# First output projection: weight sums and splits made ahead during the front and the scans, kept in DRAM, and loaded as pairs

## The chip, the cores and the metric

The kernel runs on one core of one Trainium2 chip. The metric is the device time of one execution in microseconds (us). A core has TensorE (PE in the profile: matmuls; PEld: its weight loads), VectorE (DVE), ScalarE (ACT), GpSimd (POOL) and SyncE (SP), each with a queue of its own that it works off in order, and DMA engines that move data between DRAM and the on-chip memory. A DMA is issued from an engine's queue (here SP's, and GpSimd's for those that add to what lies at the target) and then runs by itself.

## What is computed

One step of a small hybrid model: an SSD (Mamba-2) layer, then a pooling layer, over 1024 prompt tokens and 64 sample tokens (1088 columns), with a model width of 1024 and an inner width of 2048. What matters here is the first layer's branch, and of it the last line:

```python
def ssd_branch(h, conv_prev, ssm_prev, w_in, ..., norm_g, w_out):
    zxbcdt = h @ w_in
    ...
    xbc_act = jax.nn.silu(conv)
    ...
    y, new_ssm = ssd_scan(xs, dt, A, Bm, Cm, ssm_prev)
    y = (y + d_skip[:, None] * xs).reshape(b, L, D_INNER)
    gated = (y * jax.nn.silu(z)).reshape(b, L, N_GROUPS, D_INNER // N_GROUPS)
    gated = gated * lax.rsqrt(jnp.mean(gated * gated, axis=-1, keepdims=True) + EPS)
    gated = gated.reshape(b, L, D_INNER) * norm_g
    return gated @ w_out, new_conv, new_ssm
```

The result is gated and added to x; then comes the pooling layer with its own output projection.

## The kernel before

*Number format.* Every float32 product is made of three: an operand is split into hi and lo, and hi·hi, hi·lo and lo·hi are added up. So each weight that TensorE uses has to be split first: a copy to hi on ScalarE, and raw minus hi on VectorE gives lo.

*The output projections* are made by a Strassen scheme of seven half-size products, in the order of ORDER, (2, 6, 3, 5, 1, 4, 7). Each product needs a weight block that is a quadrant of the weights or a sum or difference of two (WBLOCKS: a sum for 2, 5 and 1, a difference for 6 and 7, a plain quadrant for 3 and 4). Each product has four blocks, d = 0 to 3, so there are 28 blocks n = 4 x (place in ORDER) + d, each 128 partitions x 8 x 128 float32 (512 KB). A block is used by 48 matmuls with 128x128 weights, 272 columns wide: 8 rows of the block, two tiles of columns, three products.

*How a weight block is made.* `ow_fetch` loads the quadrant (SP, L1119) into a raw buffer of tag wr (three of them). `ow_add`, if the block is a sum, adds the second quadrant by a DMA that adds to its target (GpSimd's queue, L1137); if it is a difference, ScalarE first negates the raw block in place (L1135, waiting for the load). `ow_split` makes hi on ScalarE (L1148) and lo on VectorE (L1149) into the buffers wh and wl, two of each. `ow_next(n)`, called as TensorE goes through the blocks, splits one further block, adds and fetches what fits. Products send their results with `contribute` (L1168) to the rows of x. Both output projections use these functions: the first with the weights wout, the second, in the pooling layer, with pout (`self.ol` is 0 and 1).

*The stages.* `front` (0 to about 267 us) makes dt, the gates z, and the convolution inputs in eight pairs (the list FRONT; n counts pairs, and names such as B21, T1 or B22 are steps of a fast matrix product inside a pair). Then come eight scans, g = 0 to 7, of four steps p each (`scan`), from 267 to about 860 us; scan 6 begins at about 700 and scan 7 at about 785. A scan's own matmuls are few: transposes (tr, L101), S, and y; they wait for M (a decay matrix), xd and ea from VectorE and ScalarE, and h, the state. The gaps are filled by `fills`: the input projections for the groups ahead (tiles mm), and from the end of scan 6 on the first output products (tiles op, with operands b built from rows of the gated output that come back from DRAM, gyd). The table PACE says how many units of filler go where. After the scans `ssd_out` does the rest of the products until about 996 us, and then the pooling layer runs to the end, with its own output projection.

*What sets the order.* In the scans TensorE's order is pinned as it is written. The order on VectorE, ScalarE, GpSimd and SP is set by the framework's scheduler before the run; on the chip each engine then takes its list in order. Row buffers are 30 slots handed out first-in first-out: a new tile waits for the user before it.

## Time and profile before

The median of three runs is 1621.42 us (1621.29 to 1623.38). The profiled execution took 1624.89 us, of which the profile's span holds 1622.8.

| | before |
|---|---|
| profiled execution, its own time | 1624.89 us |
| span | 1622.8 us |
| granted TensorE clock, mean | 0.985 |
| PE / DVE / ACT / POOL busy | 1581.0 / 1245.1 / 807.6 / 460.3 us |
| chain of work that ended last, PE | 87% |
| DMA moved, hardware queue / software queue | 244.35 / 25.43 MB |

The span is cut into stages by time: up to 267 us the front, to 862 the scans, to 996 the rest of the first output projection. A view of "windows" gives, for each stretch, the busy time of each engine, the clock that TensorE was granted, and the share of the DMA engines' time; a row in which PE is not fully busy, or its clock is under 1, is a place where time can be won. A view of "waits" gives the idle time of an engine by what ended it, as "engine tile line <- engine tile line: us in total, times, longest".

### The profile page before, as it was taken

Reading aid. Unit: us, or ns where it says so; the run is one execution under the profiler, and the core shown is the slowest. Engines: PE = TensorE matmul, PEld = TensorE weight load, DVE = VectorE, ACT = ScalarE, POOL = GpSimd, SP = SyncE. Lnnn points to the kernel's source line nnn. Section 1 sums busy time; section 2 is a strip of 40 time slices with the busy share of each in tenths; the row PEclk is TensorE's granted clock in tenths of the full one; section 3 lists DMA queues with packets and bytes.
Section 4 is the critical chain, followed back from the end, with each engine's and each line's share of the span. In section 5 each row is a group of like instructions: output and inputs, shape, how many; then the busy total and the mean of one; then the engine's idle time right before and its main releaser. Section 6 shows DMA issues by size and latency. Waiting matters only on the chain.

```text
span 1622.8 us, 31026 instructions
## 1 busy us (share of the span) xinstructions
PE 1581.0 (97%) x12399; PEld 1521.3 (94%) x12399; DVE 1245.1 (77%) x1986; ACT 807.6 (50%) x1427; POOL 460.3 (28%) x500
## 2 busy tenths in 40 slices
PE   8999999999999999999799999999999999999997
PEld 6899999999999999998789989999999999999997
DVE  6875476777777777777889878888889777667876
ACT  6653335566657666666654357532323233233363
POOL 0233351212121121213101121665666630000331
PEclk9999999999999999999899999999999999999999
DMA  9422226435454463658599882132333379566673
GB/s 348 164 97 79 98 82 226 138 125 205 149 182 145 155 213 118 211 146 273 141 344 296 211 195 85 71 122 106 113 113 104 105 250 360 145 173 177 159 163 113
DMA packets 103782, 271.74 MB, mean 167 GB/s; under 512 B 17724, under 2 KB 41688, under 8 KB 103640
## 3 DMA queue, kind: packets, MB, share of 16 engines
q1 hardware_dynamic: 95576, 244.35, 43.4%
q0 software_dynamic: 8064, 25.43, 8.9%
q8 instruction: 97, 1.59, 0.4%
q14 instruction: 45, 0.37, 0.1%
HBM read 208.43 MB, written 56.86 MB: 163 GB/s over the span
## 4 chain that ended last, share of the span: by engine, by line
PE 87%; issue 4%; DVE 4%; ACT 2%; DMA 2%; POOL 1%; SPq 0%; DVEq 0%; POOLq 0%; ACTq 0%
PE st L98 29%; PE mm L98 28%; PE op L98 14%; PE y L98 3%; PE pl L98 3%; PE S L98 2%; PE am L98 2%; PE tr L101 1%; PE tr L98 1%; PE ms L98 1%; DMA x<-xT 1%; PE p L98 1%; DMA wr<-wout 0%; DVE rst L1315 0%; PE Z L98 0%
## 5 line engine op out<-in xcount | busy, mean ns | idle before, releaser
L98 PE MATMUL op<-b,w 128*128 128x272 f32 x2688 | 349.6, 291 | 10.9 <-ACT w L1148 5.3
L98 PEld LDWEIGHTS op<-b,w 128*128 128x128 f32 x2688 | 343.3, 191 | 16.2 <-ACT w L1148 6.0
L98 PE MATMUL st<-hh,w 128*128 128x272 f32 x1408 | 273.8, 289 | 0.0
L98 PE MATMUL mm<-hh,wh 128*128 128x364 f32 x720 | 246.8, 343 | 0.0
L98 PE MATMUL mm<-hl,wh 128*128 128x364 f32 x720 | 236.9, 329 | 0.0
L98 PE MATMUL mm<-hh,wl 128*128 128x364 f32 x720 | 236.7, 329 | 0.0
L98 PEld LDWEIGHTS st<-hh,w 128*128 128x128 f32 x1408 | 224.6, 188 | 0.3 <-issue 0.3
L98 PE MATMUL st<-t,w 128*128 128x272 f32 x1584 | 205.3, 287 | 0.0
L98 PE MATMUL st<-hl,w 128*128 128x272 f32 x704 | 203.4, 289 | 0.0
L98 PEld LDWEIGHTS st<-t,w 128*128 128x128 f32 x1584 | 201.0, 188 | 0.0
L98 PEld LDWEIGHTS mm<-hh,wh 128*128 128x128 f32 x720 | 135.8, 189 | 14.0 <-issue 9.7
L187 ACT ACTIVATE w<-wr 128x512 fp32r<-128x512 f32 x88 | 55.5, 631 | 176.3 <-PE st L98 143.0
L98 PEld LDWEIGHTS mm<-hl,wh 128*128 128x128 f32 x720 | 135.9, 189 | 0.7
L98 PEld LDWEIGHTS mm<-hh,wl 128*128 128x128 f32 x720 | 135.8, 189 | 0.0
L98 PEld LDWEIGHTS st<-hl,w 128*128 128x128 f32 x704 | 132.6, 188 | 0.0
L579 POOL TENSOR_TENSOR hd<-h,cd 128x256 f32<-128x256 f32 x56 | 70.7, 1262 | 116.1 <-ACT cd L560 58.4
L1168 DVE SCALAR_TENSOR_TENSOR x<-op,gat,x 128x272 f32<-128x272 f32 (+1 forms) x160 | 72.7, 478 | 34.5 <-PE op L98 31.4
L358 DVE SCALAR_TENSOR_TENSOR raw<-raw,vec,raw 128x1112 f32<-128x1112 f32 x64 | 90.3, 1411 | 10.0 <-ACT raw L356 9.7
L363 POOL COPY ncv<-raw 128x3 f32<-128x3 f32 x32 | 17.1, 533 | 277.9 <-ACT raw L433 267.0
L1148 ACT ACTIVATE w<-wr 128x1024 fp32r<-128x1024 f32 x56 | 59.0, 1054 | 69.1 <-PE op L98 55.0
L946 DVE TENSOR_TENSOR u<-st,u 128x272 f32<-128x272 f32 (+1 forms) x158 | 61.4, 409 | 40.1 <-PE st L98 38.1
L189 POOL TENSOR_TENSOR w<-wr,w 128x512 fp32r<-128x512 f32 x44 | 79.5, 1806 | 37.9 <-ACT w L187 37.6
(272 smaller groups left out, 3216.9 us busy)
## 6 DMA issues: line engine op xcount, KB each, us to landing
wr<-win SPq DMA_DIRECT2D x48, 512.0 KB, 4.0
acb<-acd SPq DMA_DIRECT2D x32, 512.0 KB, 3.8
wr<-pin SPq DMA_DIRECT2D x32, 512.0 KB, 3.5
wr<-wout SPq DMA_DIRECT2D x28, 512.0 KB, 6.5
wr<-pout SPq DMA_DIRECT2D x28, 512.0 KB, 4.6
row<-gyd SPq DMA_DIRECT2D x22, 544.0 KB, 6.7
wr<-wout POOLq DMA_DIRECT2D x20, 512.0 KB, 8.3
wr<-pout POOLq DMA_DIRECT2D x20, 512.0 KB, 5.9
```

What stands on the lines that cost most here:

```text
L98: return self.pin(self.build.nc.tensor.matmul(*a, **k))
L101: return self.pin(self.build.nc.tensor.transpose(*a, **k))
L187: self.nc.scalar.activation(hi, src, AF.Copy)
L189: eng.tensor_tensor(out=lo, in0=src, in1=hi.bitcast(F32), op=ALU.subtract)
L358: nc.vector.scalar_tensor_tensor(out=acc[:, :n], in0=raw[:, k:k + n], scalar=w[k], in1=acc[:, :n], op0=ALU.mult, op1=ALU.add)
L363: nc.gpsimd.tensor_copy(ncv[:, 0:1, :], raw[:, 1024:1027].unsqueeze(1))
L579: nc.gpsimd.tensor_tensor(out=hd, in0=h, in1=cd[:, :, cc].unsqueeze(2).to_broadcast([P, 4, 64]), op=ALU.mult)
L946: nc.vector.tensor_tensor(out=out, in0=x, in1=y, op=ALU.add)
L1148: self.nc.scalar.activation(hi, r, AF.Copy)
L1168: ins = nc.vector.scalar_tensor_tensor(out=x[e][:, a:a + pn], in0=ps[:, :pn], scalar=g, in1=x[e][:, a:a + pn], op0=ALU.mult, op1=ALU.add)
```

## The change

The 28 blocks of the first output projection are no longer made when they are needed. Each is made in two halves ("pieces" of 128 x 4 x 128, 56 in all) beside earlier work:

- `prep_start(n)` takes a slot for each of n pieces and loads one or two quadrant halves (SP, 256 KB each; 96 loads in all).
- `prep_end()` finishes the pieces that were started before: VectorE adds or subtracts the two halves where the block is a sum or difference (40 of 56), ScalarE copies to hi, VectorE makes lo, SP stores hi and lo together (512 KB) to a DRAM tile wpd, and the slot comes free.
- `front` calls them in pairs 1 to 4, and `scan` twice in each step of scans 0 to 5 (the table PREP gives the counts).
- `ow_load()` loads a block's hi and lo from DRAM, 512 KB each, into the seven buffers that were wr (3), wh (2) and wl (2). In the first projection `ow_next(n)` calls it until blocks up to n + 2 are requested. `ow_fetch`, `ow_add` and `ow_split` are left to the second projection.

Gone from the first projection are so 28 loads of wout on SP, 20 adding DMAs on GpSimd, 8 negations and 28 copies on ScalarE, and 28 subtractions on VectorE; the line numbers behind the functions move by two to 48.

```diff
+PREP = {(g, p): (1, 1 if p < 3 or g == 0 else 0) for g in range(6) for p in range(4)}
+OWTAGS = ("wr", "wr", "wh", "wl", "wr", "wh", "wl")
...
+    def prep_start(self, n):
+
+        for _ in range(min(n, 56 - self.prepn)):
+            i, h = divmod(self.prepn, 2)
+            self.prepn += 1
+            blocks, op = WBLOCKS[ORDER[i // 4]]
+            t = self.slots.get("wp", F32R)
+            v = t[:, :1024].rearrange("p (i k m) -> p i k m", i=2, k=4)
+            for j, b in enumerate(blocks):
+                self.nc.sync.dma_start(v[:, j].bitcast(F32), self.io["wout"][i % 4 + 4 * b[0]][:, 8 * b[1] + 4 * h:8 * b[1] + 4 * h + 4, :])
+            self.preps.append((i, h, op, t, v))
+
+    def prep_end(self):
+
+        nc = self.nc
+        for i, h, op, t, v in self.preps:
+            if op:
+                nc.vector.tensor_tensor(out=v[:, 0].bitcast(F32), in0=v[:, 0].bitcast(F32), in1=v[:, 1].bitcast(F32), op=op)
+            nc.scalar.activation(v[:, 1], v[:, 0].bitcast(F32), AF.Copy)
+            nc.vector.tensor_tensor(out=v[:, 0], in0=v[:, 0].bitcast(F32), in1=v[:, 1].bitcast(F32), op=ALU.subtract)
+            nc.sync.dma_start(self.wpd[i][:, :, 4 * h:4 * h + 4, :], v.bitcast(F32))
+            self.slots.free(t)
+        self.preps = []
+
+    def ow_load(self):
+
+        n = len(self.owsplit)
+        if n >= 28:
+            return
+        w = []
+        for i in range(2):
+            tag = OWTAGS[(2 * n + i) % 7]
+            t = self.wp.tile([P, 8, P], F32R, tag=tag, bufs=3 if tag == "wr" else 2, name=self.name("w"))
+            self.nc.sync.dma_start(t.bitcast(F32), self.wpd[n][:, 1 - i])
+            w.append(t)
+        self.owsplit.append(w)
...
     def ow_next(self, n):
 
-        for _ in range(2 if self.ol and n > 21 else 1):
+        while not self.ol and len(self.owsplit) < min(28, n + 3):
+            self.ow_load()
+        for _ in range(0 if not self.ol else 2 if n > 21 else 1):
             self.ow_split()
...
+                if 0 < n < 5 and x in ("B21", "T1", "B22"):
+                    self.prep_end()
+                    if x != "B22":
+                        self.prep_start(2)
...
             if j == 4:
-                for _ in range(2):
-                    self.ow_fetch()
-                self.ow_add()
+                self.ow_load()
...
-        self.ow_split()
-        self.ow_fetch()
-        self.ow_add()
+        self.ow_load()
...
             a, b, c = PACE[g][p]
+            pa, pb = PREP.get((g, p), (0, 0))
+            self.prep_end()
+            self.prep_start(pa)
             self.units(fill, a)
...
+            self.prep_end()
+            self.prep_start(pb)
             self.units(fill, b)
```

Three places show how the engines' lists change. The first is **VectorE in scan 2** (between 440 and 475 us before the change): cb, M (L561) and ea (L562) feed TensorE's y, xd (L545) its S and y, and xbc L587 takes y up. Before:

```order
L548 TENSOR_TENSOR cb_4975<-tr_4950,kc 128x256
L587 SCALAR_TENSOR_TENSOR xbc_4310<-xbc_4310,vec,y_5032 128x256
L561 TENSOR_TENSOR M_4979<-M_4979,cb_4975 128x1024
L587 SCALAR_TENSOR_TENSOR xbc_4531<-xbc_4531,vec,y_5032 128x256
L562 TENSOR_TENSOR ea_5155<-xbc_4132,ea_5155 128x1024
L732 SCALAR_TENSOR_TENSOR xbc_3523<-xbc_3523,vec,rs_5063 128x1088
L732 SCALAR_TENSOR_TENSOR xbc_3742<-xbc_3742,vec,rs_5063 128x1088
L545 TENSOR_TENSOR xd_5137<-tr_5127,tkx 128x2x256
```

With the change:

```order
L550 TENSOR_TENSOR cb_5221<-tr_5196,kc 128x256
L1145 TENSOR_TENSOR wp_5192<-wp_5192 128x512
L563 TENSOR_TENSOR M_5225<-M_5225,cb_5221 128x1024
L1147 TENSOR_TENSOR wp_5192<-wp_5192 128x512
L589 SCALAR_TENSOR_TENSOR xbc_4514<-xbc_4514,vec,y_5285 128x256
L589 SCALAR_TENSOR_TENSOR xbc_4749<-xbc_4749,vec,y_5285 128x256
L1145 TENSOR_TENSOR wp_5868<-wp_5868 128x512
L564 TENSOR_TENSOR ea_5415<-xbc_4322,ea_5415 128x1024
L1147 TENSOR_TENSOR wp_5868<-wp_5868 128x512
L547 TENSOR_TENSOR xd_5397<-tr_5387,tkx 128x2x256 x2
```

Two pieces have come between (a sum, L1145, and a subtraction, L1147, of each): one around M, one around ea, ahead of the next xd; the two operations with rs (L732) have left this place for a later one in the scan.

The second is **ScalarE ahead of scan 7**, about 769 to 788 us before the change: M (L557) is followed by the silu (L394, with its table load) that makes xbc for the scan, and then by b, the hi copies of the output product's operands (L1088). Before:

```order
L356 ACTIVATE raw_8584<-raw_8347,vec 128x1112
L557 ACTIVATE M_8774<-acb_8344,tka_1657 128x128 x4
L557 ACTIVATE M_8774<-acb_8344,tka_1658 128x128 x4
L1135 ACTIVATE wr_8610<-wr_8610 128x1024
L1148 ACTIVATE w_8679<-wr_8597 128x1024
L394 ACT_TABLE_LOAD
L394 ACTIVATE xbc_8583<-xbc_8583 128x1088
L1088 ACTIVATE b_8639<-raw_8600 128x544
```

With the change:

```order
L358 ACTIVATE raw_8971<-raw_8735,vec 128x1112
L559 ACTIVATE M_9148<-acb_8732,tka_1719 128x128 x4
L559 ACTIVATE M_9148<-acb_8732,tka_1720 128x128 x4
L713 ACTIVATE z_8827<-xbc_7869 128x1088
L396 ACT_TABLE_LOAD
L396 ACTIVATE xbc_8970<-xbc_8970 128x1088
L1090 ACTIVATE b_9018<-raw_8984 128x544
```

The negation and the copy of a weight are gone from ahead of the table load, and one square of the gated output (L711 before, L713 now; it stood some 15 rows later) has come there.

The third is **SP's list in scan 2**, at the same time: acb (L519, broadcast decays for M and ea), win (weights of the input projection), rsd and rs (the gate's scale to DRAM and back) and z. Before:

```order
L519 DMA acb_4993<-acd 128x4x256
L132 DMA wr_5175<-win 128x1024
L704 DMA z_5274<-zsd_133 128x1088
L724 DMA rsd_122<-z_4467 4x272
L727 DMA rs_5063<-rsd_122 128x1088
L519 DMA acb_5171<-acd 128x4x256
```

With the change:

```order
L521 DMA acb_5239<-acd 128x4x256
L1137 DMA wp_5868<-wout 128x512
L1137 DMA wp_5192<-wout 128x512 x2
L134 DMA wr_5442<-win 128x1024
L1148 DMA wpd_169<-wp_5192 256x1x512
L726 DMA rsd_122<-z_4685 4x272
L1148 DMA wpd_172<-wp_5868 256x1x512
L729 DMA rs_5316<-rsd_122 128x1088
L1137 DMA wp_5384<-wout 128x512 x2
L521 DMA acb_5431<-acd 128x4x256
```

Loads and stores of pieces now stand between the same transfers; rs and the next acb come behind two stores that wait for VectorE's subtractions, and z has moved behind them.

More of the change, by code (lines that the diff above doesn't have):

```diff
@@ L1123, in ow_src @@
     def ow_src(self, d, b):
-        return self.io[("wout", "pout")[self.ol]][d + 4 * b[0]][:, 8 * b[1]:8 * b[1] + 8, :]
+        return self.io["pout"][d + 4 * b[0]][:, 8 * b[1]:8 * b[1] + 8, :]
+    def prep_start(self, n):
[29 more added lines that the diff above has]
+        self.owsplit.append(w)
     def ow_add(self):
@@ L1143, in ow_split @@
         r = self.owraw[n]
-        if self.ol and ORDER[n // 4] == 7:
+        if ORDER[n // 4] == 7:
             hi, lo = (self.slots.get("w", F32R)[:, :1024].rearrange("p (k m) -> p k m", k=8) for _ in range(2))
@@ L1276, in run @@
             self.b12d = [dr.tile([P, HALF], F32, tag=f"b12d{i}", name=f"b12d{i}") for i in range(8)]
+            self.wpd = [dr.tile([P, 2, 8, P], F32, tag=f"wpd{i}", name=f"wpd{i}") for i in range(28)]
+            self.preps, self.prepn = [], 0
             self.x1d = [dr.tile([P, TOK], F32, tag=f"x1d{i}", name=f"x1d{i}") for i in range(8)]
```

## The prediction

> **What bounds the kernel now.** I read four views in this order: the windows of 100 us, TensorE's own waits, the 10-us windows around each wait, and the timelines of the engines there. The columns of a windows row are stretch, its length, busy time of PE, PEld, DVE, ACT and POOL (with counts), TensorE's granted clock, DMA share and GB/s.
>
> ```profile
> 300.00:400.00 100.00, 99.92 (x844) 92.79 (x843) 77.25 (x108) 64.04 (x131) 23.25 (x37) 1.00 0.48 155
> ...
> 600.00:700.00 100.00, 100.00 (x858) 93.00 (x857) 78.10 (x111) 61.40 (x119) 20.75 (x38) 1.00 0.51 172
> 700.00:800.00 100.00, 88.52 (x673) 82.19 (x672) 76.76 (x116) 66.30 (x126) 20.76 (x30) 0.90 0.69 207
> 800.00:900.00 100.00, 94.28 (x808) 87.95 (x807) 89.21 (x167) 48.28 (x90) 12.89 (x16) 0.97 0.89 286
> 900.00:1000.00 100.00, 94.23 (x729) 92.87 (x728) 83.54 (x160) 55.47 (x85) 18.76 (x36) 0.98 0.69 178
> ```
>
> TensorE is the bound, and it cannot be relieved of work here: the change leaves its matmuls alone. What can be won is idle time and half-clock time. Scans 0 to 5 (about 267 to 700 us) have neither. From 700 to 1000, where the last two scans and the first output projection run, TensorE is idle for 300 - 277.04 = 22.96 us. Its waits there:
>
> ```profile
> PE tr L101 <- DVE xd L545: 5.4, 1, 5.4
> PE op L98 <- DVE w L1149: 3.8, 3, 2.7
> PE S L98 <- DVE xbc L587: 3.6, 1, 3.6
> PE tr L98 <- DVE xd L545: 3.2, 1, 3.2
> PE op L98 <- ACT w L1148: 3.0, 2, 1.9
> PE tr L101 <- ACT xbc L394: 2.9, 1, 2.9
> PE op L98 <- ACT b L1088: 0.9, 1, 0.9
> ```
>
> These seven rows add to 22.8 us: it is the whole idle time. Only 3.8 + 3.0 = 6.8 us of it name the weight split that the change removes. Whether the rest hangs on it too must be read place by place:
>
> ```profile
> 750.00:760.00 10.00, 6.85 (x69) 5.25 (x69) 9.49 (x15) 5.12 (x10) 3.36 (x2) 0.72 1.01 377
> 760.00:770.00 10.00, 10.00 (x84) 9.61 (x85) 8.99 (x15) 9.97 (x18) 3.83 (x5) 0.94 0.69 244
> ...
> 780.00:790.00 10.00, 5.21 (x34) 4.67 (x32) 5.13 (x9) 8.51 (x10) 0.88 (x1) 0.76 0.50 120
> 790.00:800.00 10.00, 6.47 (x30) 5.89 (x31) 9.76 (x18) 6.44 (x10) 1.48 (x2) 0.56 0.63 161
> ...
> 810.00:820.00 10.00, 7.63 (x76) 6.75 (x74) 9.05 (x16) 7.43 (x15) 2.22 (x3) 0.96 0.88 260
> 820.00:830.00 10.00, 8.79 (x56) 7.75 (x58) 9.87 (x20) 5.78 (x13) 1.72 (x3) 0.70 1.04 377
> ...
> 910.00:920.00 10.00, 10.00 (x82) 10.00 (x82) 9.35 (x19) 3.10 (x5) 0.18 (x1) 1.00 0.67 197
> ...
> 980.00:990.00 10.00, 7.26 (x58) 7.04 (x58) 9.52 (x22) 7.10 (x14) 0.45 (x2) 1.00 0.25 81
> 990.00:1000.00 10.00, 10.00 (x69) 10.00 (x69) 9.51 (x20) 6.45 (x12) 1.28 (x5) 0.83 0.54 181
> ```
>
> The clock column falls in or behind a gap. A clock c means half speed for (1 - c)/0.5 of a row; work done at half speed loses half of its time, so a row loses at most (1 - c) x 10 us, and less by half of what it was idle anyway. That is 1.8 to 3.4 us at 750 to 770, 2.6 to 6.8 at 780 to 800, 1.6 to 3.4 at 810 to 830 and up to 1.7 at 990.
>
> The largest place is 780 to 800 (8.3 us idle: the 5.4 and the 2.9). The timelines show its cause (start, length, engine, line, operation, in brackets the idle time before and what ended it); the last row, from the chain, is the transfer:
>
> ```profile
> 770.66 2.45 ACT L557 ACTIVATE M<-acb,tka 128x128 f32<-128x128 f32 x8
> 781.43 1.06 ACT L1135 ACTIVATE wr<-wr 128x1024 f32<-128x1024 f32 x1 [8.32 <-DMA wr<-wout]
> 782.40 1.04 ACT L1148 ACTIVATE w<-wr 128x1024 fp32r<-128x1024 f32 x1
> 784.75 1.11 ACT L394 ACTIVATE xbc<-xbc 128x1088 f32<-128x1088 f32 x1
> 777.26 0.28 DVE L361 SCALAR_TENSOR_TENSOR xbc<-raw,vec,raw 128x64 f32<-128x64 f32 x1
> 783.47 1.23 DVE L1149 TENSOR_TENSOR w<-wr,w 128x1024 fp32r<-128x1024 f32 x1 [4.42 <-ACT w L1148]
> 785.91 1.33 PE L101 MATMUL tr<-kc,xbc 128*128 128x128 f32 x5 [2.89 <-ACT xbc L394]
> 773.31 8.04 DMA wr<-wout
> ```
>
> ScalarE runs in order. The negation of a weight (L1135) stands ahead of the silu for scan 7 (L394), and waits 8.32 us for a weight load that SP issued only at 773.31. The xbc that the silu makes is what the transposes (L101) need, and TensorE goes idle for it at 785.91 - 2.89 = 783.0. VectorE, too, stands still for 4.42 us at a split, with the operations ahead of xd (L545) queued behind it. So these 8.3 us hang on the weights although no weight is named.
>
> **The change part by part.** Removed between 740 and 990:
>
> ```profile
> L1148 ACT ACTIVATE w<-wr x56: 1039/1060/1068, 743.5 to 1585.9; 128x1024 fp32r<-128x1024 f32 x56
> L1149 DVE TENSOR_TENSOR w<-wr,w x56: 1211/1217/1353, 763.4 to 1587.9; 128x1024 fp32r<-128x1024 f32 x56
> 815.36 1.22 DVE L1149 TENSOR_TENSOR w<-wr,w 128x1024 fp32r<-128x1024 f32 x1
> L1135 ACT ACTIVATE wr<-wr x16: 1039/1058/1062, 781.4 to 1576.5; 128x1024 f32<-128x1024 f32 x16
> wr<-wout SPq DMA_DIRECT2D x28, 512.0 KB, 6.5
> wr<-wout POOLq DMA_DIRECT2D x20, 512.0 KB, 8.3
> ```
>
> Half of the splits belong to this projection: 28 x 1.217 = 34 us of VectorE; on ScalarE 28 x 1.060 + 8 x 1.058 = 38 us; and 20 accumulating transfers. What it is worth, place by place:
> - *780 to 800.* With no L1135 or L1148 ahead, the silu waits for its own input. VectorE made that at 777.5 (L361), so the silu moves from 784.75 to about 779 at the latest, with the table load ahead of it, though one square of the gate (L711) now stands ahead too. TensorE went idle at 783, so the transposes should not wait. 8.3 us and a clock loss near 4 us are at stake. VectorE's xd still stands behind a dozen small operations of the output product, so I take **9 us** of the 12.
> - *810 to 830.* TensorE waited 3.6 us for L587, which stood behind the split at 815.36 on a VectorE busy for 9 in 10. That split goes, and one at 802; nothing comes. At stake 3.6 and about 2.5 of clock; half: **3 us**.
> - *The named waits*, in the dense stretch from 860 on: 6.8 us and up to 1.7 of clock at 990. What is late next is the ready load: two of 512 KB for each block of 48 matmuls (about 6.2 us of TensorE), issued up to two blocks ahead, about 12 us, against 6.5 us from issue to landing in the row above. I take **6 us**.
> - *747 to 770.* This wait (3.2) follows the longest wait of VectorE for the gate's scale, rs, on its way back from DRAM (the L732 row below: 5.9 us); its place in VectorE's order stays. **0**.
>
> Together 18 us of the 22.96 idle and 8 to 15 of clock.
>
> Added ahead, in front pairs 1 to 4 and scans 0 to 5: 56 pieces of 128x512. The same shapes stand in the trace:
>
> ```profile
> L187 ACT ACTIVATE w<-sw x66: 615/631/635, 98.1 to 1328.6; 128x512 fp32r<-128x512 f32 x66
> L189 DVE TENSOR_TENSOR w<-sw,w x66: 674/693/1785, 99.0 to 1329.3; 128x512 fp32r<-128x512 f32 x66
> DVE xbc L732 <- DMA rs<-rsd: 18.9, 6, 5.9
> ACT ea L552 <- DMA acb<-acd: 13.1, 9, 3.2
> L579 POOL TENSOR_TENSOR hd<-h,cd x56: 607/1553/1685, 285.0 to 838.1; 128x256 f32<-128x256 f32 x56
> ```
>
> VectorE: 40 sums and 56 subtractions x 0.693 = 66.5 us. ScalarE: 56 x 0.631 = 35 us. A scan of 71 us takes about 7 pieces: 7 x (40/56 + 1) x 0.693 = 8.3 us on VectorE, from 77% to 89%, and 4.4 us on ScalarE, from 64% to 70%. So VectorE does 66.5 - 34 = 32 us more in all, in a stage where TensorE has not waited once. At 910 to 920 VectorE is busy for 9.35 of 10 and TensorE for all 10, at 760 to 770 for 8.99 and TensorE again all 10; at 810 to 820 it is 9.05 and TensorE loses 2.4. So 89% may cost nothing or a wait. Lower bound 0; upper bound one wait like the 3.6 with its 2.5 of clock in each of six scans, 36 us. VectorE's idle time in a scan (22.5% of 71 us, 16 us) is twice what comes, so I take the near end, **2 us** in all.
>
> SP's queue gets 96 loads of 256 KB and 56 stores of 512 KB, about 6.8 MB in a scan, 96 GB/s on top of 155 to 172. A store waits for VectorE's subtraction, and behind it stand acb, rs, z and h0 loads of the scan. If one is late by the 3.2 us that ScalarE has already waited for acb, TensorE's lead has covered it so far. From nothing to 3.2 us in each of six scans, 19 us; near the lower end, **0.5 us**.
>
> The Trainium skill ("SBUF — State Buffer", section on the two separate sides) speaks against the change: a VectorE operation with two SBUF inputs and a GpSimd one that reads SBUF exclude each other for a whole instruction. The L189 row agrees in its longest (1785 ns against 693). By that rule, as an estimate, 96 operations that meet GpSimd in a fifth of cases for half of L579's 1.55 us add 15 us of VectorE time; the rows by themselves, at the median, add none. Spread over the stage it is 2 to 3 us a scan, and still below VectorE's idle time.
>
> The profiled execution took 1624.89 us (span 1622.8 and 2.1 around it): 1624.9 - 18 + 2.5 = 1609.4. It lay 3.5 us above the median of 1621.42; from the median the forecast is **1606 us**.
>
> **The rivals.**
> 1. *Swallowed.* Other work takes over in the same places: xd behind the product's own VectorE work at 780 to 800, L587 at 810, and the ready loads (twice the requests on SP, in order with rows and x1d stores) in place of the split. For it: DMA share 1.04 at 820 to 830. Against it: the accumulating transfers, 8.3 us each, go. It leaves only about 5 us: **1616 us**.
> 2. *Slower.* VectorE falls behind in scans 0 to 5. The pieces stand between cb and M and ahead of ea, which feed the y matmuls; TensorE's order is fixed, so one late y stops everything. At the upper bound above, 36 us against 18: **1639 us**. It decides from 18/6 = 3 us a scan on. Against it: no wait of TensorE at all in 300 to 700.
> 3. *The loads are not ready*, so that the change does not do what it says: the pairs come from DRAM later than the split would have been done. If each of 28 blocks waited 1 us, 28 us against 18: about 1631 us. Against it: 12 us ahead for 6.5 us.
>
> **How the numbers follow.** The forecast's own case, 8 to 27 us gained, gets 0.70; the first rival 0.16, the second 0.10, the third 0.04. Below 26 us of gain (all idle time but the 3.2, and 6 of clock; 1595 us) lies perhaps 0.05; above 1626 most of the last two rivals. So the range is 1595 to 1626. A difference under 0.2% (3.2 us) is about what a measurement of this kernel cannot tell from none. Faster: 0.70 and 0.09 of the first rival, 0.79; within 0.2%: 0.07 of it and 0.02 of the others, 0.09; slower 0.12.
>
> **What would show it.** Right: the 100-us rows from 300 to 700 keep TensorE at 99.9 or more with VectorE at 87 to 90; ScalarE shows no wait near 780; TensorE is idle under 10 us in 700 to 1000, and the clock at 780 to 800 is near 1; the wait near 750 stays. The software queue falls by 20 x 0.524 = 10.5 MB and the hardware queue grows by 25.2 + 29.4 + 29.4 - 14.7 = 69 MB. Wrong: TensorE waits for M, ea, xd or h before 700 with a clock below 1 there (second rival), or for a load of ready weights after 770 (third), or L545 and L587 still stop it at 780 to 830 (first).

## The result, and the profile after

The changed kernel takes 1647.07 us (median of 4 runs, 1646.3 to 1652.09) against 1621.36 us before: ratio 1.0162, 95% interval 1.0141 to 1.0184. It is 25.7 us slower, where the prediction had 15 us faster and a range of 1595 to 1626. The profiled execution took 1647.45 us, its span 1645.5, so 22.7 us more than the span before.

The page of the change, engine line and DMA queues:

```profile
PE 1585.4 (96%) x12399; PEld 1524.2 (93%) x12399; DVE 1275.6 (78%) x2054; ACT 800.3 (49%) x1447; POOL 439.7 (27%) x480
...
q1 hardware_dynamic: 128664, 313.57, 55.9%
q0 software_dynamic: 5184, 14.94, 5.2%
```

The work is what was worked out: the queues moved by +69.2 and -10.5 MB, VectorE does 30 us more, GpSimd 21 less. Only the waits are elsewhere. To see where, both programs are cut at the same events. The first state copy of a scan (VectorE, h<-S) is one; here scans 0, 6 and 7, first before, then with the change:

```profile
284.54 0.41 DVE L576 COPY h<-S 128x256 f32<-128x256 f32 x1
...
711.10 0.42 DVE L576 COPY h<-S 128x256 f32<-128x256 f32 x1
...
798.41 0.42 DVE L576 COPY h<-S 128x256 f32<-128x256 f32 x1
```

```profile
301.55 0.41 DVE L578 COPY h<-S 128x256 f32<-128x256 f32 x1
...
742.40 0.42 DVE L578 COPY h<-S 128x256 f32<-128x256 f32 x1
...
818.01 0.42 DVE L578 COPY h<-S 128x256 f32<-128x256 f32 x1
```

Scan 0 begins 17.0 us late; by scan 6 the delay is 31.3; scan 6 gives back 11.7. In the table each column is a stage between such events, in us longer (+) or shorter (-) than before: the front, scans 0 to 6, scan 7 with the dense rest of the output projection (to the first matmul of pl, the pooling layer), the pl matmuls, and all that follows. The rows below the first are the experiments. All are single profiled executions, within 6.5 us of the medians. The one of the kernel before lay 3.5 us above its median, so the table shows losses too small, and gains too large, by about as much. The two runs of the kernel before with negations moved agree with it to 1 us in the front and 0.3 us in scans 0 to 5; so most of the 3.5 us should lie in scan 6 or behind it.

| run | front | 0 | 1 | 2 | 3 | 4 | 5 | 6 | 7+out | pl | rest | span |
|---|---|---|---|---|---|---|---|---|---|---|---|---|
| before (us) | 284.5 | 69.2 | 72.2 | 70.9 | 70.9 | 71.1 | 72.2 | 87.3 | 197.7 | 49.0 | 577.7 | 1622.8 |
| the change | +17.0 | -0.4 | +4.7 | +6.7 | +2.2 | +1.1 | 0.0 | -11.7 | -1.9 | +4.9 | +0.1 | +22.7 |
| pieces in scans only | -0.5 | +0.4 | +10.1 | +4.4 | +0.6 | +0.8 | +0.4 | -11.8 | -2.0 | +4.9 | +0.7 | +8.1 |
| pieces in front only | +16.2 | -0.4 | 0.0 | 0.0 | 0.0 | -0.3 | +0.2 | -11.2 | 0.0 | +3.4 | -0.5 | +7.4 |
| no loads | +4.5 | -2.3 | +3.9 | 0.0 | +1.8 | +1.7 | -0.1 | -11.4 | +0.7 | +3.4 | +1.4 | +3.5 |
| transfers only | +4.4 | +0.2 | +17.9 | +6.3 | +2.7 | -0.2 | -0.1 | -11.4 | +1.3 | +3.4 | -0.5 | +24.1 |
| 56 pieces in scans 0 to 6 | +0.1 | +0.3 | +11.7 | +0.6 | +4.2 | +2.1 | +5.6 | +1.6 | -2.1 | +3.4 | -0.2 | +27.5 |
| the same, finished later | -0.1 | 0.0 | +3.6 | +7.4 | +1.4 | +1.9 | +3.9 | -11.6 | -2.1 | +4.9 | +2.3 | +11.6 |
| copies, not paced | +59.3 | +4.1 | +16.5 | 0.0 | 0.0 | -0.3 | 0.0 | -11.5 | 0.0 | +4.8 | +1.4 | +74.3 |
| copies, paced, scans | +0.9 | +3.5 | +1.1 | +0.9 | 0.0 | -0.3 | +5.5 | -11.9 | -2.4 | +4.9 | +1.0 | +3.2 |
| operations only, scans | +0.3 | +2.3 | +2.4 | 0.0 | +0.8 | +0.7 | +0.6 | -11.8 | -1.8 | +4.9 | +2.2 | +0.6 |
| scans, half the ready loads | +0.2 | +0.3 | +10.3 | +5.5 | 0.0 | +0.5 | +1.0 | -11.0 | -8.4 | +2.5 | +3.0 | +3.8 |
| scans, stores on GpSimd | +1.4 | +2.2 | +6.0 | +14.4 | +5.9 | +3.1 | -1.1 | -10.7 | -1.6 | +4.9 | +0.4 | +24.8 |
| scans, all on GpSimd | +14.1 | +0.2 | +19.2 | +10.9 | +18.0 | +9.3 | -1.4 | -11.5 | -0.7 | +3.4 | +1.4 | +63.0 |
| before, negations on GpSimd | -0.7 | -0.3 | 0.0 | 0.0 | 0.0 | -0.3 | 0.0 | -5.9 | +3.0 | -0.1 | +5.1 | +0.8 |
| the same, first projection | -1.0 | +0.1 | 0.0 | 0.0 | 0.0 | -0.3 | 0.0 | -6.5 | +2.4 | -0.1 | +1.8 | -3.6 |
| 8 blocks, scans 4 and 5 | -0.4 | -0.3 | 0.0 | 0.0 | +0.2 | +0.7 | +4.4 | -13.6 | -7.3 | +3.4 | 0.0 | -12.9 |
| 8 blocks, scans 2 to 5 | +1.6 | -0.3 | 0.0 | 0.0 | +1.0 | +0.8 | -0.9 | -11.6 | -5.4 | +5.7 | +1.6 | -7.5 |

**The front.** Windows of 100 us (columns as in the prediction), first two of the kernel before, then those of the change:

```profile
100.00:200.00 100.00, 100.00 (x800) 99.07 (x799) 55.33 (x108) 35.90 (x64) 41.91 (x32) 1.00 0.28 98
200.00:300.00 100.00, 100.00 (x770) 98.73 (x769) 66.62 (x104) 48.60 (x87) 30.58 (x35) 1.00 0.44 148
```

```profile
100.00:200.00 100.00, 90.21 (x692) 88.21 (x692) 64.35 (x117) 37.65 (x69) 34.53 (x25) 0.95 0.66 213
200.00:300.00 100.00, 97.85 (x750) 96.87 (x749) 69.21 (x113) 45.26 (x77) 35.75 (x41) 1.00 0.51 173
300.00:400.00 100.00, 100.00 (x819) 93.34 (x818) 83.60 (x123) 68.60 (x145) 23.45 (x33) 1.00 0.74 249
400.00:500.00 100.00, 94.22 (x773) 87.17 (x772) 82.68 (x119) 63.59 (x127) 20.46 (x33) 0.96 0.78 255
...
600.00:700.00 100.00, 97.65 (x788) 89.81 (x778) 83.40 (x118) 65.09 (x139) 21.25 (x33) 0.98 0.70 228
```

VectorE of the change is busy for 64% from 100 to 200, and TensorE is idle for 9.8 us there all the same, where before it was full. The waits of VectorE from 100 to 290 us, those of SP, and a piece of the timeline say why:

```profile
DVE wp L1145 <- DMA wp<-wout: 27.0, 7, 5.5
```

```profile
SPq L1148 <- DVE wp L1147: 29.7, 8, 7.5
```

```profile
154.04 0.78 DVE L948 TENSOR_TENSOR z<-st,u 128x272 f32<-128x272 f32 x2
157.98 0.69 DVE L1145 TENSOR_TENSOR wp<-wp 128x512 f32<-128x512 f32 x1 [3.16 <-DMA wp<-wout]
...
163.97 0.70 PE L100 MATMUL tr<-kc,dt 128*64 128x128 f32 x4 [6.77 <-DVE tka L508]
```

VectorE is not full: it stands still, in order, at a sum whose load has not landed. The small operations that TensorE needs (z, tka) stand behind it. And SP stands still, in order, at a store whose subtraction VectorE has not reached, with the next loads behind it. So a load, the sum that needs it and the store behind the sum wait for each other in turn.

**The scans.** From 290 to 700 us, where TensorE did not wait before, its waits in the change, ScalarE's wait for loads of pieces, and SP's waits:

```profile
PE am L100 <- ACT mp L268: 5.8, 2, 4.0
PE tr L100 <- DVE xd L547: 2.4, 1, 2.4
```

```profile
ACT wp L1146 <- DMA wp<-wout: 20.1, 7, 6.1
```

```profile
SPq L1148 <- DVE wp L1147: 73.0, 23, 8.4
...
SPq L1137 <- DMA wpd<-wp: 38.3, 11, 6.2
...
SPq L615 <- DMA wpd<-wp: 14.6, 7, 4.8
...
SPq L706 <- DMA wpd<-wp: 11.2, 5, 2.5
```

A piece of the chain (start, length, what):

```profile
456.35 5.34 DMA wpd<-wp
...
468.74 4.64 DMA wp<-wout
...
473.50 0.70 DVE wp L1145
...
479.08 0.54 SPq L1148
...
483.39 7.45 DMA wp<-wout
...
490.94 0.18 ACT wp L1146
...
496.73 0.28 ACT mp L268
...
497.06 1.03 PE am L100 x4
```

SP stands 73.0 us at stores of pieces (L1148) that VectorE has not finished. A load of a piece (L1137) waits on SP until the last store out of its slot has landed; so do loads of h0 (L615) and z (L706) that got such a slot. The end of this chain is ScalarE at a piece whose load landed at 490.84, with mp (adaLN) behind it, and TensorE waits 4 us for mp. Transfers of pieces are 17 of the 41 us of this chain by the rows shown (5.34 + 4.64 + 7.45).

**The gain.** TensorE's only long wait in scan 6 of the change, then the windows there:

```profile
PE tr L103 <- DVE xd L547: 3.5, 1, 3.5
```

```profile
802.00:812.00 10.00, 8.80 (x72) 8.61 (x70) 10.00 (x20) 8.52 (x12) 0.00 (x0) 1.00 0.72 231
812.00:822.00 10.00, 7.66 (x79) 6.63 (x79) 9.49 (x19) 3.53 (x9) 1.77 (x1) 1.00 0.49 175
```

Of 8.3 us idle and about 4 of clock, 3.5 idle are left and the clock stays at 1.

**The dense rest.** No weight split is waited for any more, and nothing is gained. TensorE's waits from 818 to 1014 us of the change, the windows at them, and the transfer behind the second:

```profile
PE op L100 <- ACT b L1090: 5.8, 2, 5.0
PE S L100 <- DVE h L698: 4.3, 1, 4.3
```

```profile
840.00:850.00 10.00, 8.06 (x62) 7.59 (x64) 8.70 (x14) 4.96 (x13) 1.24 (x2) 0.67 1.00 369
...
960.00:970.00 10.00, 6.13 (x26) 5.59 (x27) 5.47 (x11) 5.33 (x10) 2.58 (x3) 0.66 0.95 219
```

```profile
946.02 7.41 DMA row<-row
```

The waits for splits went (ready weights are waited for 0.6 us); an operand b whose adding DMA (row<-row, 7.4 us) comes late took their place, with the clock at 0.66 behind it, and in scan 7 the state h took the place of L587. In the pl stage, 4.9 us longer, TensorE waits 1.9 us for ss (L1283) and 1.0 us for wl (L155), for which it did not wait before; every run built on the change is 2.5 to 5.7 us longer there, also those that load half the ready weights or those of 8 blocks only. What makes these late is open.

### The profile page after: what moved, and what is told of

Same layout as the page of the kernel before. It is cut to its first block, busy times and chain, and to the rows that moved or that the text cites. A ratio compares the mean times of both kernels' runs of the same rounds, so it can differ in the third digit from the quotient of the medians.

```text
span 1645.5 us, 31414 instructions
## 1 busy us (share of the span) xinstructions
PE 1585.4 (96%) x12399; PEld 1524.2 (93%) x12399; DVE 1275.6 (78%) x2054; ACT 800.3 (49%) x1447; POOL 439.7 (27%) x480
## 4 chain that ended last, share of the span: by engine, by line
PE 59%; DVE 12%; DMA 11%; issue 10%; ACT 5%; POOL 2%; SPq 1%; DVEq 0%; ACTq 0%; POOLq 0%
PE st L100 22%; PE mm L100 19%; PE op L100 9%; DMA wp<-wout 4%; DMA wpd<-wp 2%; PE y L100 2%; PE am L100 1%; PE S L100 1%; PE pl L100 1%; PE tr L100 1%; PE tr L103 1%; DVE x L1209 1%; PE ms L100 1%; DMA wr<-win 1%; DMA wr<-pout 1%
## 5 line engine op out<-in xcount | busy, mean ns | idle before, releaser
L100 PE MATMUL op<-b,w 128*128 128x272 f32 x2688 | 349.3, 291 | 10.5 <-ACT b L1090 5.8
L100 PEld LDWEIGHTS mm<-hh,wh 128*128 128x128 f32 x720 | 136.6, 190 | 13.8 <-issue 11.2
L581 POOL TENSOR_TENSOR hd<-h,cd 128x256 f32<-128x256 f32 x56 | 77.1, 1376 | 138.1 <-DVE h L582 57.9
L360 DVE SCALAR_TENSOR_TENSOR raw<-raw,vec,raw 128x1112 f32<-128x1112 f32 x64 | 89.6, 1400 | 10.1 <-ACT raw L358 9.9
L559 ACT ACTIVATE M<-acb,tka 128x128 f32<-128x128 f32 x256 | 80.5, 389 | 17.5 <-PE y L100 15.2
L1146 ACT ACTIVATE wp<-wp 128x512 fp32r<-128x512 f32 x56 | 35.0, 629 | 107.6 <-DVE wp L1145 68.4
```

What stands on the lines that cost most here:

```text
L100: return self.pin(self.build.nc.tensor.matmul(*a, **k))
L360: nc.vector.scalar_tensor_tensor(out=acc[:, :n], in0=raw[:, k:k + n], scalar=w[k], in1=acc[:, :n], op0=ALU.mult, op1=ALU.add)
L559: nc.scalar.activation(M[:, r, t], acb[:, r, t], AF.Relu, bias=self.tka[cc][:, col + r:col + r + 1], scale=-1.0)
L581: nc.gpsimd.tensor_tensor(out=hd, in0=h, in1=cd[:, :, cc].unsqueeze(2).to_broadcast([P, 4, 64]), op=ALU.mult)
L1146: nc.scalar.activation(v[:, 1], v[:, 0].bitcast(F32), AF.Copy)
```

## The experiments

Each run is timed against the kernel before on the same chip. Where a run leaves out or changes a part of the computation, its expectation says so.

### Which stage, and which part of a piece

**Pieces in scans only, pieces in the front only.**

```diff
-        for _ in range(min(n, 56 - self.prepn)):
+        for _ in range(min(n, 40 - self.prepn)):
...
-            self.nc.sync.dma_start(t.bitcast(F32), self.wpd[n][:, 1 - i])
+            self.nc.sync.dma_start(t.bitcast(F32), self.wpd[n if n < 20 else n - 8][:, 1 - i])
...
-                if 0 < n < 5 and x in ("B21", "T1", "B22"):
-                    self.prep_end()
-                    if x != "B22":
-                        self.prep_start(2)
```

> The change without its pieces in the front: the scans make 40 pieces (20 blocks), blocks 20 to 27 load the pairs of blocks 12 to 19 once more (same traffic, other numbers). From the traces, scan 0 began 17 us later than before and scans 1 to 4 took 14 us longer, while scan 6 and the dense stretch gave back about 13. If the loss of the front belongs to the pieces there: 1647 - 17 = 1630 us, with TensorE's waits of 120 to 250 us gone. Rival (the loss is a matter of DMA traffic or queues at large and moves elsewhere when the pieces move): over 1640.

```diff
-PREP = {(g, p): (1, 1 if p < 3 or g == 0 else 0) for g in range(6) for p in range(4)}
+PREP = {}
...
+            self.nc.sync.dma_start(t.bitcast(F32), self.wpd[n % 8][:, 1 - i])
```

> The change with its 16 pieces in the front alone, none in the scans; every block from 8 on loads the pair n modulo 8 (same loads in the dense stage, other numbers). If front and scans lose apart from each other: 1647 - 14 = 1633 us, with scans 1 to 4 at their 71 us again and the front still 17 us late. If the scans were slowed only as an after-effect of the front: about 1647 still, or scans still at 73 to 77 us.

Measured: 1633.53 us, ratio 1.0082 (1.0062 to 1.0101), and 1635.27 us, 1.0087 (1.0072 to 1.0102). The front's 17 and the scans' 14 to 17 are separate losses; each stays whole when the other is gone.

**No loads, and transfers only.** The expectations from here on go by letters. W: engines that work in order stand still for loads of pieces. V: the added operations cost their own time on VectorE. S: SP's queue and the slots are what is short. D: the traffic or SP's queue is the loss; later it is split into T, the traffic itself makes other transfers late, and Q, SP is held at the head of its queue by a piece that cannot start.

```diff
-            for j, b in enumerate(blocks):
-                self.nc.sync.dma_start(v[:, j].bitcast(F32), ...)
...
+            c = self.kc[:, :512].rearrange("p (k m) -> p k m", k=4)
             if op:
-                nc.vector.tensor_tensor(out=v[:, 0].bitcast(F32), in0=v[:, 0].bitcast(F32), in1=v[:, 1].bitcast(F32), op=op)
+                nc.vector.tensor_tensor(out=v[:, 0].bitcast(F32), in0=c, in1=c, op=op)
...
```

> The change without the 96 loads of wout: the pieces are made of constants that lie on the chip, with the same VectorE and ScalarE operations and the same stores (other numbers). Theory W: no wait for loads is left, and the 31 us come back, 1612 to 1620 us. Theory V: the operations are all there, 1640 or more. Theory S: part of the loss stays with the stores, which still hold SP until VectorE is done, 1625 to 1640.

```diff
-            for j, b in enumerate(blocks):
+            for j, b in enumerate((blocks * 2)[:2]):
...
-            if op:
-                nc.vector.tensor_tensor(out=v[:, 0].bitcast(F32), ...)
-            nc.scalar.activation(v[:, 1], v[:, 0].bitcast(F32), AF.Copy)
-            nc.vector.tensor_tensor(out=v[:, 0], ...)
```

> The change with the transfers of its pieces alone: loads (two halves for every piece, 112 in place of 96) and stores, no VectorE or ScalarE operation on them (raw halves are stored, other numbers). Theory W (the loss is engines standing still in order for piece loads): no engine waits for a piece now, so nearly all of the 31 us come back, 1612 to 1620 us. Theory D (the traffic of 54 MB or SP's queue is the loss): it stays, 1635 or more. Half of each would be 1622 to 1635; the run without loads left 10 us of loss in front and scans, which this run then gives to the operations or to the stores' wait for VectorE.

Measured: 1628.72 us, 1.0051 (1.0036 to 1.0066), and 1652.66 us, 1.0198 (1.0180 to 1.0216). In the **front** theory W holds: the loss falls from 17 to 4.5 us when there is nothing to wait for, and to 4.4 when nobody waits; what these last 4.5 us are is open. In the **scans** W alone does not explain the loss: with no operation on the pieces (and 112 loads in place of 96) they lose 26.8 us, more than the change's 14.3. Without loads they lose 5.0. The waits of ScalarE, VectorE and SP from 350 to 470 us of the run with transfers only:

```profile
ACT ea L554 <- DMA acb<-acd: 22.9, 4, 8.7
```

```profile
DVE xbc L734 <- DMA rs<-rsd: 9.6, 1, 9.6
```

```profile
SPq L1137 <- DMA wpd<-wp: 28.8, 7, 7.2
SPq L1144 <- DMA wp<-wout: 24.5, 11, 5.9
```

SP stands at pieces for 53 of 120 us, and the scan's own transfers come late behind them: ScalarE waits 22.9 us for acb, VectorE 9.6 for rs.

### Lead, traffic, operations, queue

**A longer lead**, as a pair: all pieces in scans 0 to 6, then the same with every piece finished one call later.

```diff
+PREP = {(g, p): (1, 1) for g in range(7) for p in range(4)}
...
+        held = self.preps[len(self.preps) - self.started:]
+        for i, h, op, t, v in self.preps[:len(self.preps) - self.started]:
...
+        self.preps, self.started = held, 0
```

> All 56 pieces in scans 0 to 6, two in each step, none in the front; numbers as the reference's. It is the partner of the next run. From the run with scans only (1633.5 us, 16 us lost in scans 1 to 4): 1632 to 1640 us, if the price belongs to pieces in scans.

> The same 56 pieces in the same steps of scans 0 to 6, each finished one call (about half a step, 9 us) later, so that its load has longer to land; same operations, same transfers. Theory W: the waits for piece loads go and with them most of the scans' loss, 1615 to 1623 us. Theory V (the operations' own time on VectorE): as its partner, within 3 us. Theory S (slots are short): as its partner or slower, since a piece holds its slot longer.

Measured: 1658.5 us, 1.0227 (1.0206 to 1.0248), far over the 1632 to 1640 expected, and 1640.04 us, 1.0120 (1.0101 to 1.0138). The lead is worth 18 us, 13 of it in scan 6, where pieces stood beside the start of the output product; scans 1 to 5 still lose 18. Waiting for a load is a part, not the whole. In the front a longer lead has no result: with pieces that hold their slots a call longer there, the list of free slots runs empty.

**Traffic that waits for nothing**: copies from DRAM to DRAM in place of the pieces, first as the scheduler puts them, then queued on SP behind the scan's latest acb.

```diff
...
+            for j, b in enumerate((blocks * 2)[:2]):
+                for w in (self.wpd, self.wpe):
+                    self.nc.sync.dma_start(w[i][:, j, 4 * h:4 * h + 4, :], self.io["wout"]...)
```

> The traffic of the pieces without anything to wait for: each piece is four copies of 256 KB from DRAM to DRAM, issued by SP at the places of the loads, with no slot, no engine operation and no wait on another piece (224 copies, 59 MB in and out of the DMA engines; other numbers). The run with transfers alone lost 31 us in front and scans. Theory T (traffic as such: other transfers land later because of it): most of that loss stays, 1640 us or more. Theory Q (SP's queue in order: a piece's load at its head waits for a slot whose last store has not landed, and acb, rs and weights behind it come late): nothing of the pieces waits now, so the loss goes, 1612 to 1622 us.

```diff
...
+            with self.tc.issue_after(self.lastsp):
+                b = blocks[0]
+                for w in (self.wpd, self.wpe):
+                    self.nc.sync.dma_start(w[i][:, h], self.io["wout"][i % 4 + 4 * b[0]][:, 8 * b[1]:8 * b[1] + 8, :])
```

> Scans only, 40 pieces, and of each piece only traffic that waits for nothing: two copies of 512 KB from DRAM to DRAM, queued on SP behind the scan's latest acb load, so that they are spread over scans 0 to 5 as the pieces were (the earlier run without this order issued its copies early and crowded front and scan 0); other numbers. The run with all of the 40 pieces in scans lost 16 us in scans 1 to 5, the one with transfers alone 27. Theory T (traffic as such, acb landing in 5.6 us in place of 3.8): 12 to 27 us lost in the scans, 1628 us or more. Theory Q (SP held at the head of its queue by a piece that waits for its slot, its load or VectorE): under 5 us lost in the scans, 1610 to 1618 us.

**Operations without transfers.**

```diff
-                self.nc.sync.dma_start(v[:, j].bitcast(F32), ...)
...
-            nc.sync.dma_start(self.wpd[i][:, :, 4 * h:4 * h + 4, :], v.bitcast(F32))
+            if i < 2:
+                nc.sync.dma_start(self.wpd[i][:, :, 4 * h:4 * h + 4, :], v.bitcast(F32))
...
```

> Scans only, 40 pieces, and of each piece only its VectorE and ScalarE operations, on constants (stores of the first two blocks alone, no loads of wout; the output product loads those two blocks over and over; other numbers). Theory V (VectorE's added 0.7-us operations are late for TensorE): the 16 us of the scans stay in good part, 1622 us or more. If the operations are hidden, as the prediction had it (2 us): 1609 to 1615 us.

Measured: 1697.85 us, 1.0466 (1.0442 to 1.0490): the copies, with nothing to hold them back, crowded into the front, so that this run tells only that crowded traffic is dear. Paced: 1628.31 us, 1.0060 (1.0039 to 1.0081). Operations only: 1625.21 us, 1.0035 (1.0021 to 1.0049). A window in scan 1 and the landing of acb and win from 290 to 700 us of the paced copies, then the same window with the operations only:

```profile
350.00:420.00 70.00, 69.54 (x586) 64.06 (x585) 52.52 (x73) 42.36 (x90) 17.20 (x25) 1.00 0.85 272
```

```profile
acb<-acd SPq DMA_DIRECT2D x23, 512.0 KB, 4.6
wr<-win SPq DMA_DIRECT2D x23, 512.0 KB, 9.1
```

```profile
350.00:420.00 70.00, 68.42 (x577) 63.12 (x576) 61.79 (x91) 46.62 (x93) 17.93 (x25) 1.00 0.53 176
```

With the DMA engines at 0.85 TensorE keeps 69.5 of 70 us; with VectorE at 88% (61.79 of 70) it keeps 68.4. Over scans 0 to 5 traffic alone loses 10.7 us and operations alone 6.8, together about what the whole pieces lose (16.7); traffic alone so lies between what T and what Q gave. But not at the same place: in scans 1 and 2, where the whole pieces lose 14.5, traffic loses 2.0 and operations 2.4. Some 10 us there come with neither part by itself, while transfers that wait for slots and for each other lose 24.2 in the same two scans. That the waiting makes the difference is argued, not shown: the copies also stood at a better place in SP's queue, behind the scan's acb, and the two were not tried apart.

**Pieces off SP's queue**: stores, then loads too, issued by GpSimd.

```diff
-            nc.sync.dma_start(self.wpd[i][:, :, 4 * h:4 * h + 4, :], v.bitcast(F32))
+            nc.gpsimd.dma_start(self.wpd[i][:, :, 4 * h:4 * h + 4, :], v.bitcast(F32))
```

> As the run with pieces in scans alone (1633.5 us, 16.7 us lost in scans 0 to 5), with the pieces' stores issued by GpSimd and not by SP: same operations, same bytes, but SP is no longer held until VectorE has subtracted. Theory Q: much of the 16.7 comes back, 1620 to 1627 us, unless GpSimd's own work (hd, which the state h needs) is then late behind the stores. Theories T and V: no gain, 1632 or more.

> The same with the pieces' loads on GpSimd's queue too, so that nothing of a piece stands in SP's queue (104 issues of about 0.9 us each on GpSimd, whose idle time in scans 1 to 5 is over 75%). Theory Q: acb, rs and weights are in time, 1616 to 1624 us if hd is not held up; if GpSimd, in order too, is held by pieces as SP was, TensorE waits for h in place of the rest, 1630 or more. Theory T: 1630 or more with no wait for h.

Measured: 1651.12 us, 1.0191 (1.0154 to 1.0228), and 1690.49 us, 1.0429 (1.0410 to 1.0448). Both are worse, against theory Q as I had put it. SP's waits from 290 to 700 us with the stores on GpSimd:

```profile
SPq L1137 <- DMA wpd<-wp: 63.1, 13, 8.2
...
SPq L615 <- DMA wpd<-wp: 36.2, 9, 8.5
...
SPq L706 <- DMA wpd<-wp: 28.2, 5, 9.7
```

SP is no longer held by VectorE, but by slots: the stores leave GpSimd late, so a slot comes back late, and the next loads into it, of pieces, h0 and z, hold SP for 127 us (51 us in the run with pieces in scans only, which has the stores on SP; 64 in the change). TensorE's longest wait in total is for mp (12.7 us); for h, whose hd GpSimd makes, it waits 4.4. So the queue is the place where it shows, and what looks short is the slot, held from the load until the store has landed. This is read from the waits; a run with more slots was not made. With the loads on GpSimd too, TensorE waits for h (24.9 us), whose hd stands behind pieces there.

### The gain

**The negation alone**, in the kernel before: made by GpSimd, in both projections, then in the first alone.

```diff
-            self.nc.scalar.activation(self.owraw[n], self.owraw[n], AF.Copy, scale=-1.0)
+            self.nc.gpsimd.tensor_scalar(out=self.owraw[n], in0=self.owraw[n], scalar1=-1.0, scalar2=None, op0=ALU.mult)
```

> The kernel before, with one edit: the negation of a weight block (L1135) is made by GpSimd, whose adding DMA waits for it anyway, in place of ScalarE. It tests what the prediction said of 780 to 800 us: that the silu of scan 7 stood behind a negation that waited for its load. If so, it gains there by itself what the change gained (scan 6 was 11.7 us shorter in the change's trace): 1607 to 1613 us. If the gain came from the removal of the splits or of the weight's loads: 1617 to 1622.

> The kernel before with the negations of the first output projection alone on GpSimd (the earlier run moved those of the second projection too, and lost 5.1 us at the end there). Its scan 6 was 5.9 us shorter and the dense stretch 3.0 longer: 1620 - 3.6 = 1616 to 1618 us. If the end's loss had another cause: 1623 to 1626 again.

Measured: 1626.04 us, 1.0031 (1.0019 to 1.0044), and 1621.38 us, 0.9990 (0.9975 to 1.0006). Scan 6 gets 5.9 and 6.5 us shorter, half of what the change gains there, but the kernel gains nothing: 8.0 and 4.1 us are lost again from scan 7 on, and the profiled execution of the kernel before lay 3.5 us above its median. Neither run met its expectation. TensorE's longest wait from 690 to 1000 us in the second:

```profile
PE tr L101 <- DVE xd L545: 5.5, 1, 5.5
```

The wait for the silu went, the wait for xd stayed whole. Splits and their transfers still stand on its way, which was not tried apart. So the negation named by the trace was not the only thing in line.

**Half the ready loads** in the dense rest: a block's hi also serves as its lo.

```diff
-        for i in range(2):
+        for i in range(1):
...
-            w.append(t)
+            w += [t, t]
```

> As the run with pieces in scans alone (1633.5 us), but in the first output projection a block's hi is loaded once and used as its lo too: half the ready loads, 14.7 MB less between 750 and 990 (other numbers). In that run, as in the change's own trace, the dense stretch waited 4.5 to 5 us at about 955 for an operand b whose adding DMA row<-row came late, and 4.3 at about 835 for the state h. If the doubled weight loads make row<-row late: the wait at 955 goes, dense stretch 5 to 8 us shorter, 1626 to 1629 us. If not: 1632 to 1635.

Measured: 1628.35 us, 1.0035 (1.0015 to 1.0055). Its waits for b from 800 to 1010 us:

```profile
PE op L100 <- ACT b L1090: 0.9, 2, 0.5
```

The wait of 4.5 us is gone, and the dense rest and pl are 8.8 us shorter than with both loads (-8.4 and +2.5 against -2.0 and +4.9). By the medians it is about 7.5 us (1.0035 against 1.0082). So the loads of the ready pairs are what ate the gain there; whether by their bytes or by their requests in SP's queue was not tried apart.

**A smaller change**: the first 8 blocks (products 2 and 6) ahead, 16 pieces; the rest as before. First with the pieces in scans 4 and 5 (shown), then in scans 2 to 5 at half the rate.

```diff
+PREP = {(g, p): (1, 1) for g in (4, 5) for p in range(4)}
+READY = 8
...
+        if not self.ol and n == 0:
+            self.owraw, self.owtags, self.owadd = [None] * READY, [None] * READY, READY
...
+            if not self.ol and len(self.owsplit) < READY:
+                self.ow_load()
+                if n < READY - 4:
+                    continue
+            else:
+                self.ow_split()
```

> A smaller change: only the first 8 blocks (products 2 and 6) are made ahead, 16 pieces in scans 4 and 5, two in each step, none in the front; blocks 8 to 27 are fetched, added and split as before; numbers as the reference's. In the change's trace scans 4 and 5 lost 1.1 us with 14 pieces and scan 6 gained 11.7, while the dense stretch and the handover to the pooling layer lost 3.0. If gains and losses belong to their places: 1620 - 11.7 + 1 to 3 = 1609 to 1612 us. If pieces anywhere cost 0.3 us each as in scans 1 and 2: 1615 to 1620.

> As the run before, with the 16 pieces spread over scans 2 to 5, one in each step. If the loss comes from pieces close behind each other (a load that waits for the slot of the piece before): less loss than two in a step, 1607 to 1612 us. If scan 2 is dear as such (it lost 6.7 us in the change's trace): 1612 to 1618.

Measured: 1615.67 us, ratio 0.9958 (0.9944 to 0.9972), and 1616.39 us, 0.9966 (0.9954 to 0.9979). Both are faster than the kernel before, by 0.4 and 0.3%, and than the changed one; neither reached the 1612 us or less that they had in their better cases. The profiled execution of the first lay 4.0 us under its median, so its row in the table flatters it. Scan 6 keeps its 11.6 to 13.6 us, the pieces cost 5.1 us in scans 4 and 5, and 0.9 when spread over scans 2 to 5, and the dense rest, with the old way of making weights, is better than with ready pairs. The windows of the first of them from 600 to 800:

```profile
600.00:700.00 100.00, 99.17 (x849) 91.98 (x848) 87.22 (x123) 63.11 (x126) 23.15 (x38) 1.00 0.79 261
700.00:800.00 100.00, 94.31 (x773) 88.06 (x773) 86.11 (x135) 69.14 (x137) 18.37 (x26) 0.98 0.72 246
```

At the same DMA share (0.79) and a fuller VectorE (87%) than in the change's scans, TensorE is idle for 0.8 us in 100. It is not free for that: scan 5 of this run is 4.4 us longer, and from 700 to 710, at its end, TensorE is busy for 8.51 us at a clock of 0.83.

## Why the prediction was wrong, step by step

- *What bounds the kernel, and the idle 22.96 us*: right (the three rows add to 277.03, so 22.97).
- *780 to 800, 9 us*: right. 8.3 idle and 4 of clock, less the 3.5 left, is 8.8. The cause was half named: with the negation alone moved, scan 6 is about 6 us shorter, and the wait for xd stays.
- *747 to 770, 0*: wrong to the good side. The wait of VectorE for rs fell from 5.9 to 3.2 us, and TensorE's 3.2 to 0.3. What made rs earlier was not tried apart.
- *810 to 830 and the named waits, 3 + 6 us*: failed. "What is late next is the ready load" was the wrong answer: loads were in time (0.6 us of waits). Late next was the operand b, and half the ready loads made it early; with pl, whose part is open, the balance is +3.0 in place of -9. The first rival had the result. It named the ready loads, by their requests on SP, but xd and L587 beside them: the wait for xd fell from 5.4 to 3.5 us and that for L587 went.
- *Added ahead, 2 + 0.5 us*: the step that decides, and it is 31. Two things in it failed. First, the working priced the pieces in the **scans** alone; the front got no term and no reason for it. In the windows of before TensorE is full there and VectorE at 55 to 67%, which looks as safe as the scans. It cost 17.0. Second, the working asked whether VectorE has *time* for the pieces ("VectorE's idle time in a scan is twice what comes"), and in the main it has: operations alone cost 6.8 us over six scans, which is over three times the 2 but half of the loss; paced traffic alone cost 10.7. It didn't ask what stands in order *behind* a piece that waits. SP's wait for a store was named in it and put at 0.5 us "near the lower end", because TensorE's lead had covered such waits before; the upper end written there, 19 us, is near the 14.3 of scans 0 to 5, in part by luck: it was six times a late acb, and TensorE's named waits there are for mp, behind ScalarE at a piece whose load is late, and for xd.
- *The second rival* had the sign and the size (36 us), with VectorE too full before M and ea as its mechanism. VectorE is at 83% in place of 89, and the waits of VectorE, ScalarE and SP at pieces are for loads, slots and each other.
- *The port that VectorE and GpSimd share* (the Trainium skill, "SBUF — State Buffer", the two separate sides): the rule's estimate was 15 us of VectorE time. The pieces' sums average 798 ns and the subtractions 732 at medians of 684 and 686, so 40 x 0.114 + 56 x 0.046 = 7 us: it shows, at half the size. All ten of the 96 that took over 0.72 us ran beside an operation of GpSimd, eight of them in the front. It decides little: with the same operations and no loads the front lost 4.5 us.

Still open: how the change's own 14 us in the scans divide among traffic, operations and waits for each other. The parts were measured alone, and they don't fall on the same scans as the whole.

## What to carry to other kernels

Work moved into a stage with idle engines is not priced by its busy time alone but by what stands behind it in order while it waits: for its load, for the slot, for the store before it; look for that on the DMA-issuing queue as well as on the engines. A buffer that holds load, work and store in turn is taken for the sum of all three, and where buffers are shared, every other user of them is late too. When waits in a stage all go away and its length doesn't change, look at what the new traffic makes late; and move only the blocks whose wait was real: 8 of 28 gave 0.4%, all of them lost 1.6%.

## What the runs showed of the hardware that was not expected

With the DMA engines at a mean share of 0.81 to 0.85 from 300 to 700 us (paced copies; about 0.5 before), the median 512 KB load of win landed in 9.1 us in place of 4.5, but acb in 4.6 in place of 3.8, and two of the six scans paid nearly all of it (3.5 us in scan 0 and 5.5 in scan 5, at most 1.1 in the others). The copies that nothing held back filled 0.83 to 0.93 of the engines' time from 0 to 350 us and cost 59 us in the front. Which part of that is the higher share, and which the stage with its small operations, was not tried apart.
